# Low-rank products on the whole TensorE array, and the recurrence's outputs of a head pair in two passes

## The chip, the cores and the metric

One core of one Trainium2 chip runs one layer of a decoder as one program. The metric is the device time of one execution in microseconds (us). The kernel before takes 1330.34 us (median of three runs).

## The reference, cut to what matters

512 prompt tokens and 8 sample tokens (520 columns) go through a layer with attention, an RWKV-7 recurrence, gates and a SwiGLU network. The change touches two products of the recurrence.

```python
log_w = -jax.nn.softplus(-(lw['w0'] + jnp.tanh(xw) @ lw['w2'])) - 0.5    # w2: 64 x 1024
a = jax.nn.sigmoid(lw['a0'] + xa @ lw['a2'])                             # a2: 64 x 1024
...
def step(S, inp):                                                        # one token, 16 heads of 64
    sa = jnp.einsum('bhij,bhj->bhi', S, -kk_t)
    S = S * w_t + sa * (kk_t * a_t) + v_t * k_t
    return S, jnp.einsum('bhij,bhj->bhi', S, r_t)
```

## The kernel before

Everything is kept feature-major: 128 features in the partitions, 520 tokens in the columns, and a product takes the columns in two halves of 260. A large product is exact to more than one fp32r pass: the weights are split into a high and a low fp32r part, the activations too, and three products are summed (high by high, high by low, low by high). So a tile of 128 output features is 48 matmuls of 128 rows by 128 columns by 260 tokens. These are the filler of the whole program ("mm" in the rows).

The 16 heads are handled as 8 pairs (p = 0 to 7). A pair has a stream of steps (`pair`, `solve`, `turn_a`, `chain`) which a planner (`Weave`) puts in one order with the filler while the program is written. The planner has its own prices for instructions; an engine then runs its instructions in that order. A stream gives way at each `yield`; the planner then goes on with it, with another stream, or with six matmuls of the filler. Nearly every instruction is recorded by one helper, so all rows show line 380, and are told apart by tile names.

**Low-rank products.** `small` makes, for each half of the columns, the sum of two products. `LW` holds the high part of the 64 activations in rows 0 to 63 and their low part in rows 64 to 127. The weight tile `lwh` holds the high weight part twice, so one product of 128 rows gives high by high plus high by low. The third product is the low weight part `lwl` by the high activations: only 64 rows. The same is done for `LA`. A pair has 4 products of each kind, so the program has 32 low ones.

**Outputs.** The recurrence goes over 8 chunks of 64 tokens. After it, `chain` computes the outputs of all chunks in one PSUM bank `ch`: for each chunk two products of 128 rows by 64 columns (`GH` by `GH`, one per head), and from the second chunk on two products of 64 by 64 (`AR` by `AR`, the state before the chunk). Each fp32 product of this kind stands as two matmul instructions in the trace.

```python
zw = small([(hi[:, 0], LW), (lo[:64, 0], LW)])        # L1131, in pair(p)
...
for c in range(NC):                                   # L1381, in chain(p)
    if c and c % 2 == 0:
        yield ()
```

The weight parts of the low-rank products share one buffer per part: `lwh` and `lwl` have one place each, which all gates (`gates2`) and then all pairs use in turn.

Of the kernel before, what the change touches and what calls it, by code (L numbers as in the profile page):

```python
# [8 lines left out]
FP = mybir.dt.float32  # L9
# [7 lines left out]
T = 512           # prompt tokens  # L17
NS = 8            # sample tokens
NT = T + NS
CH = NT // 2      # columns of one product  # L20
# [4 lines left out]
HB = 16           # RWKV heads  # L25
NP = HB // 2      # RWKV head pairs
HA = 8            # attention heads
C = 64            # WKV chunk
NC = T // C
TB = NT // 5      # tokens of a statistics block  # L30
# [22 lines left out]
TURNS = 4       # us  # L53
L_SEM = 0.2        # us


# ------------------------------------------------------------------ host layout
# [20 lines left out]
def _kt(w, n_out=128):  # L78
    """[K, N] -> [N/128, 128 p, K/128, 128 c]"""
    k, n = w.shape  # L80
    return np.ascontiguousarray(
        w.reshape(k // 128, 128, n // n_out, n_out).transpose(2, 1, 0, 3)
    )


def _feat(v):
    """[N] -> [128, N/128]"""
    return np.ascontiguousarray(v.reshape(-1, 128).T)
# [38 lines left out]
def _layout(x):  # L127
# [41 lines left out]
    for g, (win, dil) in enumerate(GROUPS):  # L169
        buf = f[f"cache_kv_g{g + 1}"][0]  # L170
        rows = buf.shape[1] - dil * np.arange(128, 0, -1)
        b = buf[:, rows]                                    # [8, 128, 2, 8, 64]
        b = b.reshape(NS, 2, 64, 2, 4, 2, 64)               # b, half, key, kv, hp, h2, d
        kc.append(b[:, :, :, 0].transpose(1, 4, 3, 0, 2, 5).reshape(128, 64, 64))
        vc.append(b[:, :, :, 1].transpose(1, 4, 3, 0, 5, 2).reshape(128, 64, 64))
# [45 lines left out]
# ------------------------------------------------------------------ the program  # L221
# [4 lines left out]
class Clocks:  # L226
    """An estimate, made while the program is written, of when the engines run it"""

    def __init__(self):
        self.t = dict(PE=0.0, DVE=0.0, ACT=0.0, POOL=0.0, SP=0.0)  # L230
        self.gaps = {e: [] for e in self.t}
        self.work = []
        self.tick, self.columns, self.hot = 0, 0.0, False
        self.done, self.used, self.prev = {}, {}, {}    # by tile: {region: (end, engine, latency)}

    @staticmethod
    def region(x):
        """first and last partition and element"""
        n = x.ap
        if x.space == DRAM:  # L240
            return 0, 1, x.offset, x.offset + sum((c - 1) * s for s, c in n) + 1
        p = x.offset // n[0][0]
        if x.space == PSUM:
            return p, p + n[0][1], 0, 1
        lo = x.offset % n[0][0]
        return p, p + n[0][1], lo, lo + sum((c - 1) * s for s, c in n[1:]) + 1
# [9 lines left out]
    def free(self, name, engine, r=None):  # L256
        """when a tile, or its place, may be written"""
        if name not in self.done and name in self.prev:
            name, r = self.prev[name], None
        return max(self.last(d.get(name, {}), engine, r) for d in (self.done, self.used))  # L260

    def at(self, x, engine="PE"):
        """when a tile's data is there, or its place is free"""
        n = x.name
        return self.last(self.done[n], engine, self.region(x)) if n in self.done else self.free(n, engine)

    def place(self, engine, start, price):
        """the first time from start on at which an engine is idle for long enough"""
# [17 lines left out]
    def beat(self, t, work=0.0):  # L286
        """the tensor engine's clock: full in a tick of 3.41 us if the rows were busy for 3/8 of the one before"""
        while t >= (self.tick + 1) * 10.24 / 3:
            self.tick += 1
            self.hot, self.columns = self.columns >= 1.275, 0.0  # L290
        self.columns += work

    def warmth(self):
        """the share of the last window of the tensor engine's clock gate in which its rows were busy"""
        t = self.t["PE"] - 3.4
        while self.work and self.work[0][0] < t:
            del self.work[0]
        return sum(w for _, w in self.work) / 3.4
# [11 lines left out]
class Pool:  # L310
    """a pool of tiles whose places the clocks know"""
# [12 lines left out]
    def next(self, tag, bufs):  # L324
        """when the next tile's place is free"""
# [4 lines left out]
class Unit:  # L330
    """an engine whose instructions the clocks follow"""
# [53 lines left out]
class Weave:  # L385
    """Puts the streams of a program in one order. A stream yields what its next step needs: tiles whose
    data must be there, flags, or functions that give a time. The main stream fills in wherever no other is
    ready, and in any case often enough to keep the tensor engine at its full clock."""
# [66 lines left out]
class Job:  # L455
    """One 128-column tile of a product: weights, operand (a function), what to do with the result"""
# [9 lines left out]
def program(tc, I, O):  # L466
# [3 lines left out]
    # the tensor engine takes its instructions in the order in which they are written  # L470
# [40 lines left out]
    # ---- weights: a 128-column tile as an exact sum of two fp32r parts  # L511
# [14 lines left out]
    class Part:  # L526
        """a half of OB, by its pairs as they come"""
# [64 lines left out]
    def rsqrt(p, x, shape, pre=None, tags=None):  # L592
        """1/sqrt(x) on DVE: a first guess from the exponent, then Newton's steps"""
# [13 lines left out]
    # ---- RMS norm: statistics of token blocks of tb, r spread over the partitions  # L607
    def norm_r(p, accs, sl, tb, pre):
        """stream; puts 1/rms of the tokens of sl into banks: [(first, last, bank)]"""
# [25 lines left out]
    # ---- memory  # L635
# [21 lines left out]
    # ================================================================ x and its norm  # L657
# [44 lines left out]
    half = cp.tile([128, 4, 8], FP, name="half")     # w0/2, a0/2, 1-k_a/2, k_a/2  # L702
# [22 lines left out]
    # ================================================================ attention  # L725
# [47 lines left out]
    def plain(g, kind, n):  # L773
        """the first products take x before its norm is known"""
# [117 lines left out]
    # sample tokens' attention: partition (key half, head of pair, pair, token)  # L892
    def sample_group(g):
# [57 lines left out]
        # the groups, then the key halves  # L951
# [31 lines left out]
    # ================================================================ RWKV-7  # L983
# [68 lines left out]

    def small(prods):
# [40 lines left out]
    # ---- one head pair, up to its chunk matrices  # L1094
# [27 lines left out]
    def pair(p):  # L1122
# [4 lines left out]
        hi, lo = lora_split(rw["lw", p])  # L1127
# [3 lines left out]
        zw = small([(hi[:, 0], LW), (lo[:64, 0], LW)])  # L1131
# [4 lines left out]
        za = small([(hi[:, 1], LA), (lo[:64, 1], LA)])  # L1136
# [4 lines left out]
        # 1/|kk|^2 of the prompt's tokens, by (head, token of the chunk)  # L1141
# [9 lines left out]
        # decay  # L1151
# [23 lines left out]
        # kk = k k_k, not yet of length 1;  u = 2 a kk;  k' = k (1 + (a - 1) k_a)  # L1175
        AR = r2.tile([128, 2, NC, C], FP, name=nm("AR"), tag="AR", bufs=4)
        # B, K, and B again for the second head, whose halves stand the other way round
# [18 lines left out]
        # chunk products: by head, rows (B, s) and (K, s) for the first, (K, s) and (B, s) for the second  # L1196
# [57 lines left out]
        # the values take the place of the strict part of K's rows; what they give without the state takes theirs  # L1254
# [9 lines left out]
    # ---- (I - L)^-1 of 32-blocks by forward substitution, then to 64  # L1264
    def solve(p):
# [8 lines left out]
        # partition: column modulo 4, block  # L1274
# [55 lines left out]
    # ---- the recurrence over chunks  # L1330
    def turn_a(p):
        """the removal keys token-major"""
# [12 lines left out]
    def chain(p):  # L1345
# [34 lines left out]
        ps = cbank(p)  # L1380
        for c in range(NC):  # L1381
            if c and c % 2 == 0:
                yield ()
            y = slice(c * C, (c + 1) * C)
            for i, h in enumerate(H):
                E.matmul(ps[h, y], lhsT=GH[i][:, c, C:], rhs=GH[i][:, c, 0:C], start=True, stop=(c == 0))
            if c:
                for h in H:
                    E.matmul(ps[h, y], lhsT=AR[h, 1, c], rhs=AR[h, 0, c - 1], start=False, stop=True)
# [3 lines left out]
        # group norm over the 64 values of a head, token-major  # L1393
# [80 lines left out]
    # merge of the attention groups' prompt parts by their maxima and sums: rows (class, head)  # L1474
# [58 lines left out]
    # ---- sample tokens of one pair: the state transposed, partition (head of pair, key)  # L1533
    def sample_wkv(p):
# [3 lines left out]
        else:  # L1538
            # by (head, operand, token), the heads from rows 0 and 32 on; and by (key, token, head, operand)
# [54 lines left out]
        # group norm, output  # L1594
# [21 lines left out]
    # ================================================================ gates, projections  # L1616
# [114 lines left out]
    def wo_post(n):  # L1731
        def post(ps):
# [3 lines left out]
            # the first tiles of the next product take x2 before its norm is known  # L1736
# [69 lines left out]
    # the last norm, by halves of the tokens  # L1806
# [12 lines left out]
    # ================================================================ all tiles in their order  # L1819
# [48 lines left out]
    def more():  # L1868
        """the next tile of a head pair if there is room for it, or else one of the gates"""
# [9 lines left out]
    # the first two tiles take the last head pair when the others are through  # L1879
# [73 lines left out]
```

## Time and profile before

| what | value |
|---|---|
| timed runs | 1328.23, 1330.34, 1332.32 us (median 1330.34) |
| span of the profiled execution | 1324.3 us |
| PE busy, DVE busy, ACT busy | 97%, 64%, 46% of the span |
| granted TensorE clock, mean | 0.986 |

The span reaches from the first to the last instruction of the program. The profiled execution has no time of its own in the list of runs; the median of the timed ones is 6.0 us above its span, and that difference is taken as what lies around it. PE is TensorE's matmul row, PEld its weight loads, DVE VectorE, ACT ScalarE, POOL GpSimd. In a list in order of time, the difference of two starts is what a matmul costs the stream behind it; its own duration includes the way through the array and overlaps with the next. A group written as 64*128 64x260 has 64 rows, 128 columns of weights and 260 moving columns.

### The profile page before, as it was taken

What the parts mean: (1) busy time and instruction counts of PE and PEld (TensorE: products, weight loads), DVE (VectorE), ACT (ScalarE), POOL (GpSimd) and SP (SyncE); (2) the same over time, 40 slices, a digit from 0 to 9 for tenths busy, and PEclk for the clock granted to TensorE, in tenths of its full rate; (3) what the DMA queues carried; (4) which work ended last, traced back from release to release, by engine and by line L of the source; (5) the groups of instructions that cost most, each with busy time, mean ns of one, the idle gap of its engine ahead of it and who ended that gap; (6) DMA issues with size and microseconds to landing.
All of it is one profiled execution on the core that took longest, in us unless ns stands there. A gap on an engine that the chain in (4) does not pass through costs nothing.

```text
span 1324.3 us, 29469 instructions
## 1 busy us (share of the span) xinstructions
PE 1288.9 (97%) x11738; PEld 1207.3 (91%) x11738; DVE 844.3 (64%) x2221; ACT 610.6 (46%) x1554; POOL 172.4 (13%) x260
## 2 busy tenths in 40 slices
PE   7999999999999999999999999999999999999996
PEld 6998999989989888888888888999999999999996
DVE  6957866954779988888887555655844443432333
ACT  6244254276656655677676475333432222222220
POOL 1300100100222332121123122120100000000000
PEclk9999999999979989999999899999999999999998
DMA  6523644743244554452345344552232222233331
GB/s 217 159 87 107 207 170 147 221 140 136 82 123 131 149 153 136 140 167 86 87 145 174 105 150 152 171 206 97 75 101 96 84 93 96 96 91 89 89 100 65
DMA packets 92138, 169.49 MB, mean 128 GB/s; under 512 B 42416, under 2 KB 47568, under 8 KB 92000
## 3 DMA queue, kind: packets, MB, share of 16 engines
q1 hardware_dynamic: 60880, 102.46, 25.0%
q0 software_dynamic: 14512, 46.47, 11.6%
q10 hardware_dynamic: 16608, 18.68, 4.3%
q8 instruction: 92, 1.51, 0.5%
q14 instruction: 46, 0.38, 0.1%
HBM read 133.20 MB, written 27.94 MB: 122 GB/s over the span
## 4 chain that ended last, share of the span: by engine, by line
PE 70%; DVE 12%; issue 9%; DMA 4%; ACT 3%; POOL 1%; SPq 1%; ACTq 0%; DVEq 0%; POOLq 0%
PE mm L380 54%; PE ax L380 9%; PE ch L380 7%; DVE wlo L380 2%; DMA sw<-raw 1%; DVE X L380 1%; DVE xt L380 1%; DVE qk L380 1%; SPq L380 1%; DVE raw L380 1%; DMA raw<-w_in 1%; DVE sw L380 1%; DMA fb<-FD 1%; DMA tmp<-OAD 1%; DVE k L380 1%
## 5 line engine op out<-in xcount | busy, mean ns | idle before, releaser
L380 PE MATMUL mm<-hh,whi 128*128 128x260 f32 x1136 | 341.6, 301 | 0.0
L380 PE MATMUL mm<-hh,wlo 128*128 128x260 f32 x1136 | 326.8, 288 | 2.9 <-DVE wlo L380 2.9
L380 PE MATMUL mm<-hl,whi 128*128 128x260 f32 x1136 | 326.2, 287 | 0.0
L380 ACT CAST whi<-raw 128x1024 fp32r<-128x1024 f32 (+1 forms) x165 | 170.1, 1031 | 325.2 <-PE mm L380 293.1
L380 DVE TENSOR_TENSOR wlo<-raw,whi 128x1024 fp32r<-128x1024 f32 (+1 forms) x165 | 198.1, 1201 | 138.7 <-ACT whi L380 136.5
L380 PEld LDWEIGHTS mm<-hh,whi 128*128 128x128 f32 x1136 | 216.4, 190 | 13.4 <-issue 6.0
L380 PEld LDWEIGHTS mm<-hh,wlo 128*128 128x128 f32 x1136 | 216.4, 191 | 5.1 <-DVE wlo L380 3.9
L380 PEld LDWEIGHTS mm<-hl,whi 128*128 128x128 f32 x1136 | 216.2, 190 | 1.4 <-issue 0.2
L380 PE MATMUL mm<-h2l,whi 128*128 128x260 f32 x608 | 171.5, 282 | 0.0
L380 PE MATMUL mm<-h2h,wlo 128*128 128x260 f32 x608 | 171.4, 282 | 0.0
L380 PE MATMUL mm<-h2h,whi 128*128 128x260 f32 x608 | 171.4, 282 | 0.0
L380 PEld LDWEIGHTS mm<-h2h,wlo 128*128 128x128 f32 x608 | 114.5, 188 | 0.0
L380 PEld LDWEIGHTS mm<-h2l,whi 128*128 128x128 f32 x608 | 114.4, 188 | 0.0
L380 PEld LDWEIGHTS mm<-h2h,whi 128*128 128x128 f32 x608 | 114.4, 188 | 0.0
L380 PE MATMUL mm<-fh,wlo 128*128 128x260 f32 x388 | 109.6, 282 | 0.0
L380 PE MATMUL mm<-fl,whi 128*128 128x260 f32 x388 | 109.5, 282 | 0.0
L380 PE MATMUL mm<-fh,whi 128*128 128x260 f32 x388 | 109.5, 282 | 0.0
L380 PEld LDWEIGHTS mm<-fh,whi 128*128 128x128 f32 x388 | 73.1, 188 | 0.0
L380 PEld LDWEIGHTS mm<-fl,whi 128*128 128x128 f32 x388 | 73.0, 188 | 0.0
L380 PEld LDWEIGHTS mm<-fh,wlo 128*128 128x128 f32 x388 | 72.9, 188 | 0.0
L380 DVE TENSOR_TENSOR xt<-X,LT 128x54 f32<-128x54 f32 (+21 forms) x248 | 58.7, 237 | 3.9
L380 DVE TENSOR_TENSOR X<-X,xt 128x54 f32<-128x54 f32 (+21 forms) x248 | 57.5, 232 | 4.1
(388 smaller groups left out, 2613.3 us busy)
## 6 DMA issues: line engine op xcount, KB each, us to landing
raw<-w_in SPq DMA_DIRECT2D x77, 512.0 KB, 3.8
raw<-w_gate SPq DMA_DIRECT2D x22, 512.0 KB, 3.3
raw<-w_up SPq DMA_DIRECT2D x22, 512.0 KB, 3.3
raw<-w_down SPq DMA_DIRECT2D x16, 512.0 KB, 3.5
kt<-kcache POOLq DMA_DIRECT2D x24, 256.0 KB, 3.7
kt<-vcache POOLq DMA_DIRECT2D x24, 256.0 KB, 3.7
sw<-raw ACTq DMA_DIRECT2D x64, 65.0 KB, 3.8
GD<-gt ACTq DMA_DIRECT2D x16, 260.0 KB, 2.8
```

Source lines behind the costliest of these rows:

```text
L380: r = f(*a, **k)
```

## The change

Two edits; the rest of the diff removes comments.

The low weight part of a pair's low-rank products gets a tile `lwz` of all 128 rows that is made once: GpSimd writes zeros to rows 64 to 127 when the first pair comes, and every pair writes the low part to rows 0 to 63. The low product then multiplies 128 rows, of which the lower 64 have zero weights.

The outputs are computed in two passes over the chunks: first all 16 products `GH` by `GH`, with one possible stop before chunk 4, then, after another stop, all 14 products `AR` by `AR`. Only the first chunk's products still carry the start flag; before, each chunk's first product did.

```diff
+    def lora_split2(raw):
+        hi = ep.tile([128, 2, 128], FR, name=nm("lwh"), tag="lwh")
+        S.copy(out=hi[:], in_=raw[:])
+        if "lwz" not in rw:
+            rw["lwz"] = ep.tile([128, 2, 128], FR, name="lwz", tag="lwl")
+            G.memset(rw["lwz"][64:].bitcast(FP), 0.0)
+        V.tensor_tensor(out=rw["lwz"][:64], in0=raw[:64], in1=hi[:64].bitcast(FP), op=ALU.subtract)
+        return hi, rw["lwz"]
...
-        hi, lo = lora_split(rw["lw", p])
+        hi, lo = lora_split2(rw["lw", p])
...
-        zw = small([(hi[:, 0], LW), (lo[:64, 0], LW)])
+        zw = small([(hi[:, 0], LW), (lo[:, 0], LW)])
...
-        za = small([(hi[:, 1], LA), (lo[:64, 1], LA)])
+        za = small([(hi[:, 1], LA), (lo[:, 1], LA)])
...
         for c in range(NC):
-            if c and c % 2 == 0:
+            if c == NC // 2:
                 yield ()
             y = slice(c * C, (c + 1) * C)
             for i, h in enumerate(H):
-                E.matmul(ps[h, y], lhsT=GH[i][:, c, C:], rhs=GH[i][:, c, 0:C], start=True, stop=(c == 0))
-            if c:
-                for h in H:
-                    E.matmul(ps[h, y], lhsT=AR[h, 1, c], rhs=AR[h, 0, c - 1], start=False, stop=True)
+                E.matmul(ps[h, y], lhsT=GH[i][:, c, C:], rhs=GH[i][:, c, 0:C], start=(c == 0), stop=False,
+                         skip_group_check=True)
+        yield ()
+        for c in range(1, NC):
+            y = slice(c * C, (c + 1) * C)
+            for h in H:
+                E.matmul(ps[h, y], lhsT=AR[h, 1, c], rhs=AR[h, 0, c - 1], start=False, stop=(c == NC - 1),
+                         skip_group_check=True)
```

## Rows read from the trace of the kernel before

**Rows 1.** The page: engines' busy time, and the chain that ended last by engine.

```profile
PE 1288.9 (97%) x11738; PEld 1207.3 (91%) x11738; DVE 844.3 (64%) x2221; ACT 610.6 (46%) x1554; POOL 172.4 (13%) x260
...
PE 70%; DVE 12%; issue 9%; DMA 4%; ACT 3%; POOL 1%; SPq 1%; ACTq 0%; DVEq 0%; POOLq 0%
```

**Rows 2.** Busy time by stretch: stretch, then PE, PEld, DVE, ACT, POOL; PEclk.

```profile
397.00:530.00 133.00, 128.65 (x1237) 114.22 (x1236) 120.86 (x400) 79.72 (x202) 39.20 (x57) 0.97 0.51 142
530.00:662.00 132.00, 131.51 (x1456) 114.32 (x1454) 111.19 (x381) 89.99 (x293) 24.33 (x35) 1.00 0.41 120
662.00:761.00 99.00, 97.96 (x1143) 82.96 (x1144) 69.66 (x264) 61.62 (x185) 21.93 (x32) 0.97 0.50 142
```

**Rows 3.** PE's waits, 330 to 830 us: total, times, longest.

```profile
PE ax L380 <- ACT KB L380: 2.1, 4, 0.7
```

**Rows 4.** PE in order of time, low-rank products of pair 2: start, duration, operation.

```profile
404.76 0.39 PE L380 MATMUL ax<-LW,lwh 128*128 128x260 f32 x1
405.08 0.38 PE L380 MATMUL ax<-LW,lwl 64*128 64x260 f32 x1
405.39 0.39 PE L380 MATMUL ax<-LW,lwh 128*128 128x260 f32 x1
405.71 0.38 PE L380 MATMUL ax<-LW,lwl 64*128 64x260 f32 x1
406.02 0.39 PE L380 MATMUL mm<-hh,whi 128*128 128x260 f32 x1
406.25 0.28 PE L380 MATMUL mm<-hl,whi 128*128 128x260 f32 x1
406.36 0.28 PE L380 MATMUL mm<-hh,wlo 128*128 128x260 f32 x1
```

**Rows 5.** The tile lwl: duration in ns min/median/max, first and last start.

```profile
L380 PE MATMUL ax<-tw,lwl x16: 277/283/388, 274.1 to 309.1; 128*128 128x260 f32 x16
...
L380 PE MATMUL ax<-LW,lwl x16: 380/382/584, 336.1 to 665.8; 64*128 64x260 f32 x16
...
L380 PE MATMUL ax<-LA,lwl x16: 380/382/386, 337.5 to 669.9; 64*128 64x260 f32 x16
```

**Rows 6.** PE in order of time, pair 6: a low product before the recurrence.

```profile
612.61 0.38 PE L380 MATMUL ax<-LA,lwl 64*128 64x260 f32 x1
612.92 0.27 PE L380 MATMUL ch<-VTr,GH 64*64 64x64 f32 x1
```

**Rows 7.** The tile ch: the output products GH by GH (columns as in rows 5).

```profile
L380 PE MATMUL ch<-GH x256: 222/222/270, 542.7 to 823.4; 128*64 128x64 f32 x128
```

**Rows 8.** PE in order of time, outputs of pair 1: beginning and end.

```profile
580.10 0.45 PE L380 MATMUL ch<-GH 128*64 128x64 f32 x8
580.49 0.33 PE L380 MATMUL ch<-AR 64*64 64x64 f32 x4
580.75 0.34 PE L380 MATMUL ch<-GH 128*64 128x64 f32 x4
581.01 0.33 PE L380 MATMUL ch<-AR 64*64 64x64 f32 x4
...
583.91 0.34 PE L380 MATMUL ch<-GH,KB 128*64 128x64 f32 x4
```

**Rows 9.** PE in order of time, a run of 28 matmuls of 64*64.

```profile
699.99 1.03 PE L380 MATMUL ax<-GH,AT 64*64 64x64 f32 x28
700.95 1.16 PE L380 MATMUL ax<-AR,BK 64*128 64x128 f32 x8
```

**Rows 10.** PE in order of time: a stall, with the idle time before it.

```profile
385.51 0.39 PE L380 MATMUL ax<-ident,sg 128*16 128x128 f32 x2 [1.89 <-DVE sg L380]
```

**Rows 11.** Busy time behind that stall, and in the last stage (columns as in rows 2).

```profile
385.80:396.00 10.20, 10.20 (x50) 9.32 (x50) 8.34 (x20) 2.56 (x8) 3.82 (x6) 0.50 0.36 117
...
993.00:1026.00 33.00, 33.00 (x278) 33.00 (x278) 14.01 (x21) 9.41 (x15) 0.00 (x0) 1.00 0.28 95
```

**Rows 12.** POOL in order of time, 296 to 350 us: its only entry.

```profile
335.71 2.23 POOL L380 DMA_DIRECT2D ms<-nat  x4 [67.66 <-ACT nat L380]
```

## The prediction

> **What bounds the kernel now.** I read the page first: PE is busy for 97% of the span, and 70% of the chain of waits is PE, against 12% for DVE and 3% for ACT [rows 1]. A busy PE is not a PE that does useful work, so the next view is the busy time by stretch. From 397 to 761 us, where the head pairs run, PE's row is full within some 6 us of 364, and DVE is at 91%, 84% and 70% in the three stretches [rows 2]. The list of PE's waits from 330 to 830 us says that what PE waits for is small: the largest entry is 2.1 us in four waits [rows 3]. So PE's instruction stream sets the pace of the pair stage. Behind it stands the last stage, where nothing but filler runs. A microsecond taken out of PE's stream is worth a microsecond at the end, as long as DVE, the next engine, does not step in. What the stream loses inside its "busy" time is seen only in the list in order of time, by the difference of starts.
>
> **The price of a change of shape.** In the last stage 278 matmuls of 128 rows by 128 columns start in 33.0 us, one per 0.119 us [rows 11]; 0.12 is the price of a 260-column product among its like. Around a low product of 64 rows it is another: high, low, high, low start at 404.76, 405.08, 405.39, 405.71, and the filler behind them at 406.02 and 406.25; only the one after that is back at 0.11 [rows 4]. Each product beside one of another shape costs 0.31, and the first filler 0.23. These five take 1.49 us from 404.76 to 406.25. Were all of one shape, the first would pay what the first filler pays here for following another shape (0.23), and the other four 0.12 each: 0.71. The four changes of shape cost 0.78 us, or 0.195 each.
>
> **Low products.** There are 16 for LW and 16 for LA, from 336 to 670 us [rows 5]. Each has a change before it, and one after it. I went through all 32 in the order of time: behind 25 stands a product of 128 by 128 (as in [rows 4]), so both changes vanish; behind 7 stands a recurrence product of 64 columns (as in [rows 6]), where a change stays whatever shape the low product has. 25 x 2 + 7 = 57 changes go: 57 x 0.195 = 11.1 us. That the full-array low product itself costs 0.12 can be read off the gates: their low products are already 128 by 128 and last 283 ns, as the filler does, against 382 for the 64-row ones [rows 5].
>
> Here a weight load could speak against it. If the load of the low weights had to wait for the high product because both take the same rows, a low product would start no sooner than 0.31 us after the high one, as now, and 32 x 0.19 = 6.1 us of the 11.1 would stay. The last stage says otherwise: there all loads are of the full array, are busy for all of the time that the matmuls are, and starts are still 0.119 us apart [rows 11]. The Trainium skill (TensorE: Matmul & The Clock Gate, section Part 3: Packing small matmuls) has the rule in that form: weight loads overlap with running matmuls only where the row groups differ. By that rule the time would be that of the third rival below; the trace disagrees with it, and I keep 11.1.
>
> The other pieces of this edit: DVE's subtraction goes from 128 to 64 partitions with the same 256 elements each; I take no change of its time, with bounds of none and half of it, off the path that sets the end. The zeroing on POOL is one instruction before the first pair's low product at 336 us. The gates' last low product starts at 309.1 [rows 5], so from then on the place is free, and POOL is idle until 335.71, waiting 67.66 us for ACT [rows 12]. That idle time hides it. If the order put it behind that entry, the first pair's products would be 2 to 3 us late, once. Later pairs write the tile after the pair before has read it, as they did with a place shared by all.
>
> **Outputs.** Pair 1, not interrupted: from 580.10 to 583.91, 3.81 us [rows 8]. Eight GH matmuls (two chunks, no change between) with the change behind them take 0.39; four with the change take 0.26. So four more in the same shape cost 0.13 by these rounded starts; I take 0.12. The first pass is 32 GH matmuls: 0.26 + 7 x 0.12 = 1.10. The second is 28 AR matmuls of 64 by 64; the trace has 28 of that shape in a row, from 699.99 to 700.95, 0.96 with the change behind them [rows 9]. Sum 2.06 against 3.81: 1.75 us for a pair. 256 GH matmuls are 32 for each of 8 pairs, between 542.7 and 823.4 [rows 7]: 8 x 1.75 = 14.0 us. The arithmetic and the instruction counts stay. Bounds: the new stop before chunk 4 can be used by the filler, which adds two changes; if every pair does, 8 x 0.39 = 3.1 us come off, 10.9. Upwards, nothing: the passes can't be shorter than the rows show. The stops of before let filler in too, so I take 14.0. What follows (ACT's evacuation) waits for the last product and starts 1.75 us sooner.
>
> **Sum.** 11.1 + 14.0 = 25.1 us of PE time, in a program with a span of 1324.3 us; the median of the runs is 6.0 above the span, and I leave those 6.0 as they are. What of it arrives? From 530 to 662 us lie three pairs' outputs (5.3 us) and 13 of the 57 changes (2.5 us). If PE needs 7.8 us less there, DVE's 111.2 us fall into 124.2, 90%, what it has from 397 to 530 [rows 2]. In that stretch PE is idle for 4.3 us, in the later one for 0.5 [rows 2]. I take 3.5 us as handed back to waits. Late in that case are the filler's low weight parts and the triangular solves, both on DVE. Forecast: 25.1 - 3.5 = 21.6 us, 1330.3 - 21.6 = 1308.7 us.
>
> **Rivals.**
>
> DVE takes over (18%). For it: 91% and 84% busy [rows 2]. Against it: PE's waits for DVE are few now [rows 3]. Its price: all that is gained between 397 and 662 us is handed back, 7.8 us as above and 23 changes (4.5 us) before 530. 25.1 - 12.3 = 12.8: 1317.5 us.
>
> The clock comes back (5%). It stands at 0.97 over 133 and over 99 us of the pair stage [rows 2], about 7 us at full speed. A denser stream could keep it up: 25.1 + 5 gives 1300.
>
> The weight load is exposed (6%): 6.1 us less than forecast, 1314.8 us. It is what the rule of the Trainium skill (TensorE: Matmul & The Clock Gate, Part 3) would make of it.
>
> Stalls in a new order (5%), the way to the other side. The planner sees fewer stops in the outputs and 128 rows where it saw 64, and may put products of the pairs elsewhere, before their operands are there. One such stall has a row: PE idle for 1.89 us at 385.5 [rows 10], and behind it 10.2 us at a granted clock of 0.50, the lower of the two levels, 1.2 GHz [rows 11], some 5.1 us lost; together 7.0. Three such events more than now cancel the 21.6 us, and from four on it is slower: five give 1344. Against it: in the kernel before, the whole pair stage has one stall of that size.
>
> The change does nothing (4%): the 0.31 us belong not to the shape but to the operands. Then 1330. Against it stand the same recurrence operands in runs without a change [rows 9].
>
> **How the numbers follow.** The forecast holds 62%, within 1302 to 1314 by the bounds above (25.1 and more breaks or fewer waits on the one side, 3.1 us of stops and a little more DVE on the other). The range of 8 in 10 takes in the clock at its lower end and DVE's rival and the weight load's at its upper: 1299 to 1320. About 0.3% (4 us) is what a measurement of this kernel can tell from no change. Faster than 1326.3: 62 + 18 + 5 + 6 = 91%. Same: the case without effect and one of the stall cases, 5%. Slower: 4%.
>
> **What would show it.** In the list in order of time, high and low products of a pair 0.12 us apart, and low products of 128*128 at 283 ns. For each pair, 32 GH matmuls and then 28 AR matmuls in some 2.06 us, or in two pieces with six filler matmuls between. The last stage as long as before. PE's waits from 330 to 830 us some 3 to 4 us longer; if they are 12 longer, with DVE named, it is the first rival. The prediction is wrong if the passes show more than 0.13 us for four matmuls, if the second pass waits between the two heads' products, or if PE's granted clock falls in stretches where it was full.

## The result and the profile after

The changed kernel takes 1312.19 us, the median of four runs (1307.57 to 1316.53). Its ratio to the kernel before is 0.9867, with a 95% interval of 0.9838 to 0.9896: faster by 17.7 us (13.8 to 21.6). (A fourth run of the kernel before, 1329.73 us, is in the ratio; with it the median before is 1330.03.) The forecast was 1308.7 us with a range of 1299 to 1320. The time lies 3.5 us above the forecast, and the forecast gain of 21.6 us is the upper end of that interval, so the times alone don't exclude the forecast. The execution with the profile is the longest of the four, 1316.53 us with a span of 1314.8 us.

The page's busy times and its chain by engine, to be read beside [rows 1]:

```profile
PE 1264.7 (96%) x11738; PEld 1197.5 (91%) x11738; DVE 843.7 (64%) x2221; ACT 610.6 (46%) x1554; POOL 175.0 (13%) x261
...
PE 64%; DVE 15%; issue 9%; DMA 6%; ACT 4%; POOL 1%; SPq 1%; ACTq 0%; DVEq 0%; POOLq 0%
```

The same 11738 matmuls keep PE busy for 24.2 us less, and the chain runs less through PE and more through DVE and DMA. The first sign of what comes: PE saves more than the program gains.

Low-rank products in order of time, for [rows 4] (start, duration, operation):

```profile
406.63 0.39 PE L380 MATMUL ax<-LA,lwh 128*128 128x260 f32 x1
406.86 0.28 PE L380 MATMUL ax<-LA,lwz 128*128 128x260 f32 x1
406.98 0.28 PE L380 MATMUL ax<-LA,lwh 128*128 128x260 f32 x1
407.10 0.28 PE L380 MATMUL ax<-LA,lwz 128*128 128x260 f32 x1
407.22 0.28 PE L380 MATMUL mm<-hh,whi 128*128 128x260 f32 x1
```

Only the first product pays 0.23, because a recurrence run of another shape stands ahead of it; the next three take 0.12 each, as costed. The tile `lwz`, for [rows 5] (duration in ns min/median/max, first and last start):

```profile
L380 PE MATMUL ax<-LW,lwz x16: 277/283/420, 336.7 to 664.4; 128*128 128x260 f32 x16
...
L380 DVE TENSOR_TENSOR lwz<-lwr,lwh x8: 405/408/414, 316.7 to 637.4; 64x256 fp32r<-64x256 f32 x8
L380 POOL MEMSET lwz<- x1: 307/307/307, 310.3 to 310.3; 64x256 f32 x1
```

The low product lasts 283 ns where the 64-row one lasted 382. The zeroing falls at 310.3 us, into POOL's idle time [rows 12].

The outputs of pair 1 in order of time, for [rows 8]:

```profile
569.22 1.15 PE L380 MATMUL ch<-GH 128*64 128x64 f32 x32
570.30 1.03 PE L380 MATMUL ch<-AR 64*64 64x64 f32 x28
571.26 0.39 PE L380 MATMUL mm<-hh,whi 128*128 128x260 f32 x1
```

1.08 and 0.96 make 2.04 us, against 3.81 before; all eight pairs have the 32 GH products in one piece. The tile `ch` gives the end of the pair stage, for [rows 7]:

```profile
L380 PE MATMUL ch<-GH x256: 222/222/270, 543.5 to 810.7; 128*64 128x64 f32 x128
```

The last of them starts at 810.7 instead of 823.4. Busy time by stretch, for [rows 2] (stretch, then PE, PEld, DVE, ACT, POOL; PEclk):

```profile
397.00:530.00 133.00, 124.84 (x1263) 112.58 (x1263) 123.16 (x409) 82.12 (x208) 39.57 (x57) 0.99 0.52 145
530.00:662.00 132.00, 127.81 (x1422) 113.03 (x1421) 107.74 (x371) 88.45 (x289) 25.36 (x33) 0.94 0.38 114
662.00:761.00 99.00, 95.93 (x1188) 85.05 (x1187) 74.32 (x275) 67.91 (x208) 22.46 (x35) 0.98 0.51 151
...
330.00:830.00 500.00, 474.61 (x5203) 425.83 (x5202) 396.75 (x1295) 318.05 (x942) 119.64 (x174) 0.97 0.46 135
```

PE is idle for 8.2, 4.2 and 3.1 us in the three stretches, against 4.4, 0.5 and 1.0. From 330 to 830 us it is idle for 25.4 us. The same stretch before, with 9.1 us idle:

```profile
330.00:830.00 500.00, 490.92 (x5120) 428.26 (x5120) 390.70 (x1281) 314.46 (x934) 117.06 (x173) 0.97 0.45 131
```

PE's waits in that stretch, for [rows 3] (total, times, longest):

```profile
PE ch L380 <- ACT GH L380: 4.0, 4, 2.4
PE mm L380 <- DVE wlo L380: 3.3, 4, 1.4
PE ax L380 <- DVE sd L380: 3.2, 1, 3.2
PE ax L380 <- DVE sg L380: 2.7, 1, 2.7
PE ax L380 <- ACT KB L380: 2.4, 4, 0.7
PE ax L380 <- ACT VTr L380: 2.3, 2, 1.9
```

No single wait makes the 16 us; they are many, none longer than 3.2 us, on DVE and on ACT. The stall of [rows 10] has grown:

```profile
384.55 0.39 PE L380 MATMUL ax<-ident,sg 128*16 128x128 f32 x2 [2.70 <-DVE sg L380]
```

The last stage runs at the old rate, 279 matmuls in 33 us, for [rows 11]:

```profile
983.00:1016.00 33.00, 33.00 (x279) 33.00 (x278) 14.03 (x21) 9.93 (x15) 0.00 (x0) 1.00 0.26 89
```

### The profile page after: what moved, and what is told of

It reads as the page before. It is cut to its first block, busy times and chain, and to the rows that moved or that the text cites. A ratio compares the mean times of both kernels' runs of the same rounds, so it can differ in the third digit from the quotient of the medians.

```text
span 1314.8 us, 29468 instructions
## 1 busy us (share of the span) xinstructions
PE 1264.7 (96%) x11738; PEld 1197.5 (91%) x11738; DVE 843.7 (64%) x2221; ACT 610.6 (46%) x1554; POOL 175.0 (13%) x261
## 4 chain that ended last, share of the span: by engine, by line
PE 64%; DVE 15%; issue 9%; DMA 6%; ACT 4%; POOL 1%; SPq 1%; ACTq 0%; DVEq 0%; POOLq 0%
PE mm L380 51%; PE ax L380 8%; PE ch L380 5%; DVE wlo L380 2%; DVE X L380 1%; DVE xt L380 1%; DMA fb<-FD 1%; DMA sw<-raw 1%; ACT KB L380 1%; DVE k L380 1%; DMA raw<-w_in 1%; SPq L380 1%; DVE raw L380 1%; DVE qk L380 1%; DVE GH L380 1%
## 5 line engine op out<-in xcount | busy, mean ns | idle before, releaser
L380 DVE TENSOR_TENSOR xt<-X,LT 128x60 f32<-128x60 f32 (+24 forms) x248 | 60.3, 243 | 3.6
L380 DVE TENSOR_TENSOR X<-X,xt 128x60 f32<-128x60 f32 (+24 forms) x248 | 57.6, 232 | 3.8
```

Of the source, the lines that this page charges most:

```text
L380: r = f(*a, **k)
```

## The experiments

Three theories were put to the runs. **O** (order): the planner sees other row counts and fewer stops, and the new order of instructions makes the waits. **D** (DVE): DVE is too full to deliver sooner, so PE waits for its throughput. **M** (merge): DVE's queue stands behind the loads of the attention merge, which come from a chain of transfers, so PE's arrival is early for everything behind. The rival to all three is that PE's own saving was sized wrongly.

A balance is used for several runs. It splits a profiled span into PE's idle time (span less PE busy), what the lower clock cost (the share of clock not granted, times the span) and the rest, PE's work at full clock. The clock is known to 0.001, so a difference of two works is good to some 1.3 us.

| kernel | span | clock | PE busy | PE idle | of it, 330 to 830 us | work at full clock | changes of shape |
|---|---|---|---|---|---|---|---|
| before | 1324.3 | 0.986 | 1288.9 | 35.4 | 9.1 | 1270.4 | 635 |
| the change | 1314.8 | 0.983 | 1264.7 | 50.1 | 25.4 | 1242.3 | 456 |
| the change, again | 1304.9 | 0.991 | 1255.5 | 49.4 | 23.5 | 1243.8 | 456 |
| both edits, old order | 1309.6 | 0.988 | 1263.9 | 45.7 | 16.8 | 1248.2 | 482 |
| both edits, old order, again | 1304.1 | 0.993 | 1258.6 | 45.5 | 20.5 | 1249.5 | 482 |
| old shapes, new order | 1333.7 | 0.983 | 1288.8 | 44.9 | 17.5 | 1266.1 | 618 |
| outputs alone | 1314.7 | 0.990 | 1271.8 | 42.9 | 15.7 | 1258.7 | 539 |
| low products alone | 1325.2 | 0.988 | 1278.0 | 47.2 | 20.7 | 1262.1 | 578 |
| before, lightened | 1321.4 | 0.987 | 1286.7 | 34.7 | 9.9 | 1269.5 | 627 |
| both edits, lightened | 1304.9 | 0.985 | 1261.9 | 43.0 | 18.7 | 1242.3 | 471 |
| before, no merge loads | 1322.1 | 0.989 | 1283.5 | 38.6 | 13.2 | 1269.0 | 628 |
| both edits, no merge loads | 1306.8 | 0.987 | 1263.5 | 43.3 | 17.8 | 1246.5 | 485 |
| priced | 1358.2 | 0.969 | 1283.8 | 74.4 | 34.3 | 1241.7 | 466 |

The last column counts the neighbours in PE's order whose rows or columns of weights differ (in classes of 32, 64 and 128). Each row is one execution. A row marked "again" is a second one of the same kernel; its idle time from 330 to 830 us differs from the first by 2 to 4 us.

**The order.** Four kernels ran together: the change again, unedited; both edits with the planner counting the low products as 64 rows, so that everything outside the outputs keeps its place; the old kernel with the planner counting them as 128 rows; and the outputs' edit alone.

```diff
# both edits, old order: the planner's count of a matmul's rows
-  w = ... * ins[0].partition_size() / 128
+  w = ... * (64 if ins[0].name in self.ck.thin else ins[0].partition_size()) / 128
...
+  ck.thin.add(rw["lwz"].name)
# old shapes, new order
+  w = ... * (128 if ins[0].name in self.ck.wide else ins[0].partition_size()) / 128
...
+  ck.wide.add(lo.name)
# outputs alone
-  zw = small([(hi[:, 0], LW), (lo[:, 0], LW)])
+  zw = small([(hi[:, 0], LW), (lo[:64, 0], LW)])     # lo from lora_split, as before; za likewise
```

> The changed kernel once more, beside the others on one chip. Both theories: about 1312 us, 17 to 18 us faster than before (ratio near 0.987), single runs some us apart, and PE waiting 20 to 25 us between 330 and 830 us, against 8 in the kernel before.

> Both edits, but the planner goes on counting the low products as 64 rows; outside the outputs all engines keep the order of the kernel before. Theory O (the new order costs the waits): PE's waits from 330 to 830 us fall back to 8 to 12 us and nearly all of the 25.1 us of PE time arrive: 1305 us (1302 to 1308). Theory W (DVE, ACT and POOL cannot follow a faster PE, in whatever order): waits of 20 to 25 us as in the changed kernel, 1311 to 1313 us.

> The kernel before with its old shapes (low products of 64 rows, outputs interleaved), but the planner counts the low products as 128 rows, which gives all engines the order of the changed kernel outside the outputs. Theory O: slower than before by what the order costs, 8 to 16 us, 1338 to 1346 us. Theory W: within 3 us of before, 1330 us, PE's waits as few as before.

> The two passes of the outputs alone, low products as before; the order of the other work is that of the kernel before. 14.0 us of PE time go. Theory O: all arrives, 1316 us (1314 to 1318). Theory W: the 5.3 us of the three pairs between 530 and 662 us are handed back to waits, 1321 us (1319 to 1324).

Measured: the change again 1313.56 us, ratio 0.9883 (0.9844 to 0.9922); both edits in the old order 1312.00 us, 0.9872 (0.9840 to 0.9905); the new order alone 1332.41 us, 1.0015 (0.9995 to 1.0036); the outputs alone 1318.61 us, 0.9928 (0.9899 to 0.9957). The windows from 330 to 830 us, of both edits in the old order and then of the new order alone:

```profile
330.00:830.00 500.00, 483.22 (x5273) 433.29 (x5272) 398.69 (x1305) 322.13 (x960) 118.46 (x175) 0.98 0.46 136
```

```profile
330.00:830.00 500.00, 482.55 (x5046) 419.88 (x5044) 385.94 (x1270) 310.69 (x927) 115.12 (x171) 0.97 0.45 130
```

The new order does add waits (17.5 us idle against 9.1), but it also takes 17 changes of shape away, and the work at full clock falls by 4.3 us: the two nearly cancel, and with the old order the time of both edits is the same as with the new. Theory O falls as the cause of the missing time. It may explain why the change's traces show more waits (25.4 and 23.5 us) than those of both edits in the old order (16.8 and 20.5).

**The other edit alone, and DVE relieved.** The low products' edit alone, in the old order; then the old kernel with DVE's load lightened in the pair stage. For the second, both edits lightened were meant to stand beside it, but the kernel that ran was by mistake the unlightened one of the round before: `kept_light` is both edits in the old order once more, with all the solve's steps. Its recorded expectation is for a kernel that ran only later. The last kernel gives the planner prices nearer to the rows.

```diff
# low products alone: both edits in the old order, with the old loop over the outputs
# lightened: the planner counts every step, only the first of a solve is emitted
+ ck.ghost = s > 0
  V.tensor_tensor(out=tv, in0=..., in1=..., op=ALU.mult)
  V.tensor_tensor(out=Xs[:, :m, s + 1:], in0=..., in1=tv, op=ALU.add)
+ ck.ghost = False
# priced: the change, with
- return 0.06 + n / 1200            # ACT
+ return 0.16 + n / 1200
- return max(0.054, n / 2400)       # fp32r matmul
+ return max(0.054, n / 2400 + 0.011)
+ if shape != self.ck.shape:        # rows and columns, in classes of 32, 64, 128
+     self.ck.shape, p = shape, p + 0.2
```

> The full-array low products alone, in the order of the kernel before on every engine; 57 changes of shape, 11.1 us of PE time, go. If a part of each saving is handed back to waits wherever it is made (theory W): 1324 us (1322 to 1326), since both edits in kept order gave 15 to 18 us and the outputs alone 11. If the two edits lose only together: 1319 to 1321 us.

> The kernel before with most of the triangular solves left out: of the 31 steps of each, only the first is computed, so DVE has about 110 us less to do between 400 and 780 us; the order is planned as if they were there. Both theories: PE waits little in the kernel before, so 0 to 5 us faster, 1325 to 1330 us.

> Both edits in the order of the kernel before, with the same steps of the solves left out. Theory D (it is DVE that hands time back): waits as few as in the kernel before, and the whole 25 us stand between this and the kernel before with its solves left out: 1300 to 1305 us. Theory L (waits for ACT, POOL and for the pairs' own steps, which DVE's load does not change): the difference stays 15 to 18 us, 1308 to 1314 us.

> The changed kernel with other prices in the planner: 0.1 us more for each ACT instruction, 0.011 us more for a filler product, 0.2 us for a change of shape on PE, as the traces show them. If PE's waits come from steps planned too early for ACT and DVE (theory P): waits back near 10 us and 1303 to 1306 us. If DVE simply has no room (theory D): no better than the changed kernel, 1310 to 1315 us.

Measured: the low products alone 1321.17 us, 0.9945 (0.9923 to 0.9967); the old kernel lightened 1329.78 us, 0.9992 (0.9968 to 1.0015); both edits in the old order, again, 1310.65 us, 0.9852 (0.9828 to 0.9876); priced 1357.27 us, 1.0201 (1.0171 to 1.0231).

The edits add up: 7.3 us from the ratio of the one and 9.6 from that of the other make 16.9, beside 17.0 and 19.7 for both. But the granted clock was not the same in these runs. The low products alone had a mean of 0.9886 over 12 runs, the kernel before beside them 0.9850 over 23; the outputs alone had 0.9847 against 0.9853. Taken at an equal clock, by the slope worked out below (1.05 us for each 0.001), the low products alone are 3.7 us faster (1.6 either way) of the 11.1 forecast, the outputs alone 10.4 (1.6) of the 14.0, and both edits in the old order 15.2 (1.5). By the medians the edits lose only together; at an equal clock each loses by itself, and most of what does not arrive is missing from the low products. Their window from 330 to 830 us, of one execution, points the same way, with 20.7 us idle against 9.1:

```profile
330.00:830.00 500.00, 479.33 (x5129) 423.61 (x5128) 390.18 (x1280) 315.14 (x943) 116.05 (x172) 0.98 0.45 131
```

Whether the higher clock belongs to the edit is not shown. Lightening the old kernel alone gains nothing in the median, but at a lower clock (mean 0.9815); at an equal one it is 4.7 us faster (1.6). Leaving the steps out also moved some other instructions (50 of ACT's 1554). So DVE's load held the kernel before by a few us at most, far less than the 82 us that were taken off it. The priced planner is a miss that teaches something: with 466 changes of shape, near the 456 of the change, and the same arithmetic, it is 27 us slower than before. PE's longest waits there, 330 to 830 us:

```profile
PE ax L385 <- DVE T L385: 6.9, 5, 2.5
PE ax L385 <- DVE sg L385: 4.8, 1, 4.8
PE mm L385 <- DVE ga L385: 4.5, 3, 1.7
```

So an order alone can cost more than this change gains. By the balance its work at full clock is that of the change; against the change's first profile, PE is idle for 24.3 us more over the span, and the lower clock costs 42.1 us in place of 22.4; by the slope below some 17 of the 27 us go with the clock.

**Both edits lightened, and the merge.** The lightened kernel as it was meant; both edits and the old kernel with the merge of the attention output no longer waiting for its loads; and the change with the merge moved behind the third pair.

```diff
# kept_merge, before_merge: planned as before, emitted with a constant for what the DMA brings
  V.tensor_tensor(out=av, in0=oo[...], in1=fb[:], op=ALU.mult,
+                 emit=dict(in0=smask[...], in1=smask[...]))
# merge_at2
+ MERGE_AT = 2
```

> Both edits in the order of the kernel before, with all but the first step of the triangular solves left out (the run that kept_light was meant to be). To be held against before_light, the kernel before with the same steps left out, which was as fast as the kernel before. Theory D (DVE's load hands time back): PE's idle time between 330 and 830 us falls to the 10 us of before_light and the whole 25 us arrive, 1303 to 1306 us. Theory L (waits that DVE's load in the solves does not change): 1310 to 1314 us, and an idle time of 17 to 20 us.

> Both edits in the order of the kernel before; the multiplications and sums that merge the attention groups take constants in place of the loaded sums and weights, so the same DVE work no longer waits for those loads (the output of the attention is left out by that). Theory M (the loads hold DVE's queue at 374 us, and PE's wait behind it hands back what the first two pairs' low products gave): PE idle 3 to 4 us between 330 and 397 us in place of 6 to 7, 2 to 4 us less in all: 1306 to 1310 us. Theory D: idle there stays at 6 to 7 us, 1310 to 1313 us.

> The kernel before with the same constants in the merge. Theory M: PE idles 3.1 us in that stretch in the kernel before, of which 1.9 us is the wait behind the loads; that goes, 1327 to 1329 us. Theory D: as before, 1330 us.

> The changed kernel with the merge of the attention groups (its loads, and 8 us of DVE work) moved behind the third head pair, out of the stretch where DVE is fullest. If DVE's fullness between 397 and 530 us hands time back: 1303 to 1309 us, below the changed kernel. If other waits come in the new order: 1312 to 1330 us.

Measured: both edits lightened 1303.78 us, 0.9797 (0.9769 to 0.9824); both edits without the merge's loads 1311.87 us, 0.9852 (0.9828 to 0.9875); the old kernel without them 1326.01 us, 0.9970 (0.9945 to 0.9995); merge behind the third pair 1312.43 us, 0.9878 (0.9843 to 0.9913).

Read by ratios alone, D would seem shown: lightened, the edits gain 25.9 us (0.9992 less 0.9797, of 1330), all of the PE time that was forecast. Two things speak against that reading. The first is the waits. From 330 to 830 us, the windows of the old kernel lightened and PE's longest waits in it, then the same two views of both edits lightened:

```profile
330.00:830.00 500.00, 490.12 (x5132) 428.49 (x5131) 308.35 (x807) 314.95 (x934) 118.12 (x173) 0.97 0.45 132
```

```profile
PE ax L383 <- DVE sg L383: 2.7, 1, 2.7
PE ch L383 <- ACT GH L383: 2.3, 1, 2.3
```

```profile
330.00:830.00 500.00, 481.30 (x5268) 433.05 (x5268) 318.79 (x823) 320.51 (x948) 120.40 (x177) 0.97 0.47 136
```

```profile
PE ch L384 <- ACT GH L384: 4.4, 1, 4.4
PE mm L384 <- DVE wlo L384: 3.5, 2, 2.1
PE ax L384 <- DVE sg L384: 2.7, 1, 2.7
PE ax L384 <- DVE st L384: 1.9, 1, 1.9
```

DVE is busy for some 80 us less in both than with the solves (110 had been expected), and still the edits bring 8.8 us more idle time on PE (9.9 to 18.7), about as much as in the full kernel (9.1 to 16.8 and 20.5). On DVE and ACT the two lightened kernels run in one order. So most of these waits come without a full DVE. The second is the clock. Over 120 runs of all these kernels, one common slope gives 1.05 us (standard error 0.07) of time for each 0.001 of mean granted clock. The old kernel lightened had the lower clock (mean 0.9815 over 12 runs, against 0.9867 over 6 of both edits lightened); that is lower than the kernel before's 0.9850, too, and why is not known. Taken at an equal clock the lightened pair differs by 18.8 us (2.2 either way), the pair without the merge's loads by 17.7 (2.2), and the unlightened pair by 16.1 (2.0; held against the kernel before in the last round). These are not told apart. Both kernels gain by a lighter DVE at an equal clock, the old one 4.7 us, both edits some 8. D is not borne out; whether a lighter DVE returns 2 or 3 us of the time handed back stays open.

M isn't borne out either: with constants in place of the loads the gap between new and old is no wider, and moving the merge changes nothing (1312.43). The old kernel without the loads, which by M should have lost its wait there, idles for more from 330 to 397 us, 6.5 us against 3.1. The constants also changed the order of DVE's instructions (some 270 of 2221 moved in the old kernel), so this pair tests more than the loads; in it the edits add 4.6 us of idle time (13.2 to 17.8). The idle time moved elsewhere: the window of both edits without the loads from 330 to 397 us, with 8.6 us idle against 5.9 with them (61.12 busy of 67), and PE's longest waits from 330 to 830:

```profile
330.00:397.00 67.00, 58.43 (x504) 55.62 (x503) 54.87 (x124) 38.48 (x98) 21.68 (x31) 0.93 0.45 126
```

```profile
PE mm L382 <- DVE wlo L382: 2.8, 1, 2.8
PE ax L382 <- POOL svd L382: 2.7, 1, 2.7
PE ax L382 <- DVE tmp L382: 2.3, 1, 2.3
```

No kernel of these, with all of the computation in it, is clearly faster than the change: both edits in the old order, at 1312.00 and 1310.65 us, equal it.

## Why the prediction was right, and the term that was too small

**What bounds the kernel.** Right. PE sets the pace in every version: a kernel with 82 us less on DVE is no faster in the median (0.9992) and 4.7 us faster at an equal clock, and taking work from PE's stream shortens the program.

**The price of a change of shape.** Right in the rows: 0.12 us within the shape and 0.23 behind another. In the low products alone the changes fall from 635 to 578, the 57 that were counted. The Trainium skill (TensorEngine Tiling (Array Packing), section Tiling Modes, Key Properties) says that a change of tiling mode drains TensorE. The trace agrees in that each change costs time, and the rows give the size that the page doesn't: 0.195 us.

**The two terms.** Passes of 2.04 us against the 2.06 costed; no extra stop was used, so the lower bound of 10.9 us didn't come. The balance gives 8.3 us of work for the low products alone (forecast 11.1) and 11.7 for the outputs alone (14.0), and for both in the old order 22.2, with 1.3 us of rounding in each. The second profile of it gives 20.9, the lightened pair 27.2, the pair without the merge's loads 22.5. The mean of these four is 23.2 against the forecast 25.1: right, perhaps 2 us large. The change as it was run saves more, 28.1 and 26.6, since its new order drops another 26 changes of shape (482 to 456). That part wasn't foreseen. Nor was what the new order costs, some 4 us more idle time over the span than with the old one. That the two nearly cancel is luck.

**What of it arrives.** This is the term that was mis-sized: "I take 3.5 us as handed back to waits". From 330 to 830 us PE's idle time rises by 7.7 and 11.4 us in the two profiles of both edits in the old order, by 8.8 in the lightened pair, by 4.6 in the pair without the merge's loads, and by 16.3 and 14.4 in the change; the new order with the old shapes adds 8.4 by itself, so the parts don't simply add up. (Over the whole span the first of these rises is 10.3, but 2.7 of that lie ahead of 330 us, where the edits have not begun.) The times agree: of the 23.2 us of work, 15 to 16 arrive at an equal clock, so 7 to 8 are handed back in the old order.

The place was wrong too. I looked for it from 530 to 662 us. Of the 7.7 us, 2.8 lie before 397 and 2.9 from 397 to 530 (125.76 busy of 133), and 1.0 from 530 to 662 (130.52 of 132); of the 11.4 in the second profile, 3.9, 3.0 and 2.5. And the term was taken from three pairs' outputs and 13 of the low products' 57 changes, while the low products alone bring 11.6 us more idle time (6.6 of it from 397 to 530) and the outputs alone 6.6.

The argument went by DVE's busy share. But the waits don't follow the share: they are about as large when DVE has 82 us less to do, and between a quarter (both edits in the old order) and over a third (the change) of the listed idle time is put down to ACT. They stand where an operand becomes ready at a time that PE doesn't set. The stall of [rows 10] shows it, though not as the work of the edits. Over all profiles but the priced one, it is 2.69 to 2.72 us in the six whose granted clock was 1.00 from 330 to 384 us (among them the change, both edits in the old order twice, and the old kernel lightened, which has none of the savings), and 0.72 to 2.48 in the seven where that clock was 0.97 (1.89 before). The second profile of the change is one of the seven:

```profile
387.08 0.39 PE L380 MATMUL ax<-ident,sg 128*16 128x128 f32 x2 [1.19 <-DVE sg L380]
```

So the growth of this stall from 1.89 to 2.70 goes with the clock ahead of it: time that PE gained there was in part lost in the wait. That the edits' saving is lost in the same way at other places, and that the whole of the missing time consists of such places, is argued from the lists of waits, not shown: no single wait that was removed brought it back.

**The time around the span.** The forecast left "those 6.0 as they are". The changed kernel's profiled execution has 1.8 us around its span (1316.53 against 1314.8). Every recorded run with a span of its own has 1.7 to 2.0, the kernel before included. So the profiled execution before took some 1326.1 us, 4.2 below the median, and the 6.0 was 1.8 of surroundings and 4.2 of luck. It did no harm, because the forecast subtracts from the median. It matters for the two profiles: their spans differ by 9.5 us only, the one execution being short for its kernel and the other long. The balance closes: 27.3 us of work saved (mean of two), less 14.3 more idle, is 13.0; with the 4.2 it is 17.2, beside 17.7 measured. Whether a usual execution of the kernel before has these 4.2 us as idle time or as work isn't known; as idle time, the rises above would be too large by that much.

**The rivals.** DVE takes over: its price, 12.3 us handed back, is near what the idle time shows, and the sign that the prediction named (waits 12 us longer, DVE among them) came in the change; its mechanism, DVE's throughput, is not borne out (8.8 us more idle time with 82 us less on DVE). The clock comes back: no; the granted clock of the change lies at 0.983 to 0.991 in its profiles, on both sides of 0.986, and its ten runs have a mean of 0.9857, the 61 of the kernel before beside the experiments 0.9849. The prediction named a fall of the clock where it was full as a sign of being wrong; the first profile has one, to 0.94 from 530 to 662 us, but the second has 1.00 from 530 to 830, so it does not come with every execution of the change. The weight load is exposed: no, the rows at 406.86 to 407.10 are 0.12 us apart. Here the trace speaks against the rule of the Trainium skill (TensorE: Matmul & The Clock Gate, section Part 3: Packing small matmuls) that loads overlap only where the row groups differ. Stalls in a new order: the waits came (new order alone, 8.4 us more from 330 to 830), but were mostly paid for by fewer changes of shape; the priced planner shows that the rival is real for another order (27 us, some 17 of them with the lower clock). The change does nothing: no.

## What to carry to other kernels

A lone matmul of fewer rows among full ones costs more than the same product padded with zeros, and products of one shape belong together: price the changes in the list in order of time, by differences of starts. An engine that is 97% busy doesn't pass on all that it saves: of some 25 us, 15 to 18 arrived, and the reserve is read from when its operands become ready, not from how busy the engine is that makes them. When an instruction stream is planned, a changed count in the planner is a change of its own; run the edit in the old order beside it. Before a difference of a few us is explained, hold the mean granted clocks of the two sets of runs side by side: here they took half of what one edit seemed to gain.

## What the runs showed of the hardware that was not expected

Runs of one kernel spread by more than 1% (the kernel before lies between 1320.65 and 1339.09 us in its 61 runs beside the experiments), and most of it follows the mean granted clock (0.979 to 0.990): 1.05 us per 0.001, with 2.2 us of scatter left. A difference of 0.8% between two single profiles can be nearly all clock: the two profiles of the change differ by 9.9 us of span, by 8 thousandths of clock (8.4 us by the slope), and by 0.7 us of idle time. PE's clock stood at 0.50, the lower of its two levels (1.2 GHz), for 17 us in the one:

```profile
593.90:610.90 17.00, 17.00 (x101) 14.95 (x100) 10.81 (x30) 6.49 (x15) 4.70 (x6) 0.50 0.28 84
```

In those 17 us PE had no idle time and ran 101 matmuls; the other profile of the same kernel, which has no such fall from 530 to 830 us, ran 168 from 594 to 611. Just ahead of it, from 580 to 594 us, PE was idle for 2.8 us in both. What sets the fall off in one execution and not in the next stays open.
